# Seven pairs of eleven by seven products, weight sums on GpSimd, and a first block two rows of k at a time

## Chip, cores and metric

The kernel runs on one core of one Trainium2 chip. The metric is the time of one execution on the device, in microseconds (us), as the median of three runs; less is better.

The engines are named as the profile names them: PE is TensorE (matrix products), DVE is VectorE, ACT is ScalarE, POOL is GpSimd, SP only issues transfers.

## What is computed

A decoder trunk of two layers. Each layer does a half-step SwiGLU network, a mixer (a gated recurrence beside a spatial gating branch), and another half-step SwiGLU network, each followed by a layer norm. The change is about the first half of the four SwiGLU networks, `silu(x @ a) * (x @ b)`:

```python
D_MODEL, SEQ, DEPTH, D_FF = 1024, 512, 2, 2816
def swiglu(x, w13, w2):
    a, b = jnp.split(x @ w13, 2, axis=-1)
    return (jax.nn.silu(a) * b) @ w2
for l in range(DEPTH):
    x = layer_norm(ALPHA * x + 0.5 * swiglu(x, ffn1_w13[l], ffn1_w2[l]), ln_g[l, 0], ln_b[l, 0])
    m = mixer(x, w_in[l], ...)
    x = layer_norm(ALPHA * x + m, ln_g[l, 1], ln_b[l, 1])
    x = layer_norm(ALPHA * x + 0.5 * swiglu(x, ffn2_w13[l], ffn2_w2[l]), ln_g[l, 2], ln_b[l, 2])
```

## The kernel before

**Precision.** Every factor of a product is split into a high part (ACT copies it into a rounded type, L119) and a low part (DVE subtracts, L122). A product is then three matmuls: high by high, high by low, low by high.

**A network's first half.** The 2816 columns are 22 blocks of 128, each with a weight column `a` and one `b`. Blocks k and k+11 form pair k, so there are eleven pairs. A pair is done in one of two ways. *Plain* (`plain`, L147 and L593 to L594): two blocks, each with 24 matmuls for `a` and 24 for `b`, 512 columns wide. *By seven* (`seven_pair`, `product`, L548): the block matrix product of a pair in quarters, seven products in the place of eight, each of 24 matmuls with 256 moving columns. The seven products need sums of the weight quarters and sums of the x quarters. The x sums are made once for each network (`x_sums`, L471 to L490); the weight sums once for each pair.

**The order in a network.** Pairs 8, 9 and 10 (`front`) go plain, six blocks. Then pairs 0 to 5 (`by_seven`, `S_PAIRS = 6`) go by seven. Then pairs 6 and 7 (`behind`) go plain, four blocks. Then `Seven.run` makes the second half, also by seven products, from activation sums (`activation_sums`, L330 to L335: on DVE four subtractions of 256 columns and low parts of 256 and 512 columns) and from sums of the second weights.

**Weights of a pair by seven.** `weights_of_pair` loads two tiles `ra` (each a quarter of `a` beside a quarter of `b`), and `rc` and `rd`. On DVE it makes two sums `t13` (L521, 1024 columns), two of 512 columns into `t2` (L522) and one into `rc` (L526, 1024 columns). All seven factors of a pair are split before its first product stands. Seven evictions of PSUM banks A, B, C and E on DVE (L559 to L572) and three on ACT (L557, L565, L571) put the products together.

**Sums of the second weights.** `weight_sums` makes those of three pairs on DVE, in `front`. For the other eight, `sums_in_dram` (L288) has POOL's DMA queue copy and then add, DRAM to DRAM: four groups of two pairs, six steps a group, two transfers a step. Each step waits until the one before has landed. In the program the steps stand 6 us of counted PE time apart (`SUM_GAP`, counted by `flow.tick`).

**What sets the order.** A scheduler orders each engine's queue by the program's order and by when it believes operands are ready; `keep_in_program_order` pins an instruction to its place. Each queue is served strictly in order: an instruction that waits holds back all behind it on its engine.

**The start.** `first_block` (L1018 to L1043) loads quarters of the first weights and of x in turn, runs six matmuls on zeros while it waits (L1011), and then goes over k, for each k three matmuls for `a` and three for `b` (L1041).

Of the kernel before, what the change touches and what calls it, by code (L numbers as in the profile page):

```python
# [28 lines left out]
F32 = mybir.dt.float32  # L29
# [6 lines left out]
P = 128  # L36
D = 1024
T = 512
# [45 lines left out]
def trunk(ctx: ExitStack, tc, x_in, xt_in, w13, w2, w_in, w_br, w_out, ln_g, ln_b, lb_in, hgn, sgg, sgb, sgws,  # L84
# [33 lines left out]
    def split(hi, lo, src, pinned=False):  # L118
        act = S.activation(hi, src, AF.Copy)  # L119
        if pinned:  # L120
            tc.keep_in_program_order(act)
        V.tensor_tensor(lo, src, hi.bitcast(F32), op=ALU.subtract)  # L122
# [139 lines left out]
    class Seven:  # L262
# [51 lines left out]
        def activation_sums(self, k):  # L314

            r = self.r[k]
            x = wk.tile([P, 2, 256], F32, tag="sa", name="s12", bufs=NSA)
            if k >= self.KEPT:
                hi, lo = (quads(f"t{c}{k}", F32R) for c in "hl")
                parts = hi[:, 0], lo[:, 0], hi[:, 1:3], lo[:, 1:3]  # L320
            elif self.last is None:
                hi, lo = (quads(f"t{c}{k}", F32R) for c in "hl")
                self.last = hi, lo
                parts = hi[:, 0], lo[:, 0], hi[:, 1:3], lo[:, 1:3]
            else:
# [4 lines left out]
            V.tensor_tensor(x[:, 0], r[:, 2], r[:, 3], op=ALU.subtract)  # L330
            V.tensor_tensor(x[:, 1], r[:, 0], x[:, 0], op=ALU.subtract)
            split(parts[0], parts[1], r[:, 0])
            V.tensor_tensor(r[:, 2], r[:, 0], r[:, 2], op=ALU.subtract)
            V.tensor_tensor(r[:, 0], r[:, 1], x[:, 1], op=ALU.subtract)
# [155 lines left out]
    def raw_cd(w13_of, k, early=False):  # L490

        if early:
            rc, rd = slot(f"rc{k}"), slot(f"rd{k}")
        else:
            rc, rd = (wk.tile([P, 2, 512], F32, tag="rs", name=f"r{c}{k}", bufs=2) for c in "cd")
        for z, j in enumerate((k, k + NH2)):
            nc.sync.dma_start(rd[:, z], w13_of(NF + j)[:, H[0]])
            nc.sync.dma_start(rc[:, z], w13_of(j)[:, H[1]])
        return rc, rd

    def weights_of_pair(w13_of, k, rcd=None):

        js = (k, k + NH2)
        ra = [wk.tile([P, 2, 512], F32, tag="raw", name=f"r_p{j}", bufs=NRAW) for j in js]
        rc, rd = rcd or raw_cd(w13_of, k)
        t13 = [slot(f"t13{j}") for j in js]
        t2 = slot(f"t2{k}")
        for z, j in enumerate(js):
            wa, wb = w13_of(j), w13_of(NF + j)
            nc.sync.dma_start(ra[z][:, 0], wa[:, H[0]])  # L510
            nc.sync.dma_start(ra[z][:, 1], wb[:, H[1]])

        def parts(raw, name, early=False):
            hi, lo = ((slot(f"{v}_{name}", F32R) if early else
                       wk.tile([P, 2, 512], F32R, tag="w", name=f"{v}_{name}", bufs=NW)) for v in "hl")
            split(hi, lo, raw, early)
            return [(hi[:, z], lo[:, z]) for z in range(2)]

        p = [parts(ra[z], f"p{j}") for z, j in enumerate(js)]
        for z in range(2):  # L520
            V.tensor_tensor(t13[z], ra[z], rd[:, z:z + 1].broadcast_to([P, 2, 512]), op=ALU.add)  # L521
            V.tensor_tensor(t2[:, z], ra[z][:, 0], t13[z][:, 1], op=ALU.add)  # L522
        w2 = parts(t2, f"t2{k}")
        wt = [parts(t13[z], f"t{j}") for z, j in enumerate(js)]
        w21 = parts(rc, f"c{k}", True)
        V.tensor_tensor(rc, rc, t2, op=ALU.add)  # L526
        w4 = parts(rc, f"d{k}", True)
        return p, wt, w2, w21, w4

    def seven_pair(seven, s, k, w):  # L530

        p, wt, w2, w21, w4 = w
# [7 lines left out]
        def product(ps, units, c, first=True):  # L540
            for z in range(2):
                hi, lo = units[z]
# [9 lines left out]
        A, B, C, E = (bank(f"f{c}{k}") for c in "ABCE")  # L552
        r = seven.room(k).rearrange("p q t -> p (q t)")
        lower, upper = r[:, 0:512], r[:, 512:1024]
        b0, b1 = (wk.tile([P, T], F32, tag="sa", name=f"b{c}", bufs=NSA) for c in "01")
        product(A, [p[0][0], p[1][0]], "A11")
        S.activation(upper, A, AF.Copy)  # L557
        product(B, w2, "s2")
        V.tensor_tensor(upper, upper, B, op=ALU.subtract)  # L559
        product(C, [wt[0][0], wt[1][0]], "s1")  # L560
        V.tensor_tensor(b1, C, upper, op=ALU.subtract)
        product(E, [wt[0][1], wt[1][1]], "s3")
        V.tensor_tensor(b1, b1, E, op=ALU.subtract)
        product(A, w21, "A12", False)
        S.activation(lower, A, AF.Silu)  # L565
        product(C, [p[0][1], p[1][1]], "s4", False)
        V.tensor_tensor(b0, C, upper, op=ALU.subtract)
        V.tensor_tensor(lower, lower, b0, op=ALU.mult)
        product(E, w4, "A22", False)
        V.tensor_tensor(upper, E, upper, op=ALU.add)  # L570
        S.activation(upper, upper, AF.Silu)  # L571
        V.tensor_tensor(upper, upper, b1, op=ALU.mult)  # L572

    S_PAIRS = 6

    def ffn(l, i, last=False, first_of_all=False):
# [49 lines left out]
        for z, j in enumerate(js[2:]):  # L626
            args = blocks(j)
            if z == 3:
                w = weights_of_pair(w13_of, by_seven[0], rcd)
# [3 lines left out]
            if z == 1:  # L633
                rcd = raw_cd(w13_of, by_seven[0], True)
# [5 lines left out]
        for k in by_seven:  # L640
            seven_pair(seven, s, k, w if k == by_seven[0] else weights_of_pair(w13_of, k))
        due = [front[2:] + by_seven[:2], by_seven[2:5], by_seven[5:] + behind[:1], behind[1:]]
# [361 lines left out]
    def first_block(wa, wb):  # L1004
# [5 lines left out]
        for _ in range(6):  # L1010
            PE.matmul(idle[:, 0:P], zero[:, 0:P], zero[:, 0:P], start=True, stop=True)  # L1011
# [14 lines left out]
        feature(0, 0)  # L1026
        weight(1, 0)
        feature(0, 1)
# [8 lines left out]
        for k in range(KT):  # L1037
            mh, ml = from_x(k)
            for v in range(2):
                for i, (a, m) in enumerate(((w[v][0], mh), (w[v][0], ml), (w[v][1], mh))):  # L1040
                    PE.matmul(ps[v], a[:, k * P:(k + 1) * P], m, start=(k == 0 and i == 0),  # L1041
                              stop=(k == KT - 1 and i == 2))
            flow.tick(6 * MM)  # L1043
# [107 lines left out]
```

## Time and profile before

| | us |
|---|---|
| median of three runs | 2077.43 (2075.61 to 2080.03) |
| the profiled execution | 2075.15 |
| its span, first to last instruction | 2073.4 |
| DVE busy | 1465.6 (71%) |
| ACT busy | 871.3 (42%) |
| POOL busy | 284.7 (14%) |

The span's share is that of busy time; an engine can be busy and still not be what the end waits for. The pairs by seven of the first network lie between 75.0 and 195.9 us of the span, those of the others between 764.2 and 885.1, 1104.1 and 1225.0, and 1794.0 and 1914.9: four times 120.9 us. A row of the profile reads: line, engine, operation, output and inputs with their shapes, count, busy time and mean duration, idle time ahead of it and what ended that. In a list in order of time the first number is the start and the second the duration, both in us.

### The profile page before, as it was taken

Reading aid. Unit: us, or ns where it says so; the run is one execution under the profiler, and the core shown is the slowest. Engines: PE = TensorE matmul, PEld = TensorE weight load, DVE = VectorE, ACT = ScalarE, POOL = GpSimd, SP = SyncE. Lnnn points to the kernel's source line nnn. Section 1 sums busy time; section 2 is a strip of 40 time slices with the busy share of each in tenths; the row PEclk is TensorE's granted clock in tenths of the full one; section 3 lists DMA queues with packets and bytes.
Section 4 is the critical chain, followed back from the end, with each engine's and each line's share of the span. In section 5 each row is a group of like instructions: output and inputs, shape, how many; then the busy total and the mean of one; then the engine's idle time right before and its main releaser. Section 6 shows DMA issues by size and latency. Waiting matters only on the chain.

```text
span 2073.4 us, 30387 instructions
## 1 busy us (share of the span) xinstructions
PE 2058.6 (99%) x11764; PEld 1814.0 (87%) x11764; DVE 1465.6 (71%) x2285; ACT 871.3 (42%) x1219; POOL 284.7 (14%) x424
## 2 busy tenths in 40 slices
PE   9999999999999999999999999999999999999998
PEld 7999888888888989988899998888888888899886
DVE  7986878943535788777778878779444357987776
ACT  4443555234322434446534445542343224444453
POOL 1222002001000222210112220020010002122001
PEclk9999999999999999999999999999999999999999
DMA  8788677122243578867768886861222436788674
GB/s 300 226 236 205 194 267 250 42 82 82 82 156 98 205 222 218 210 172 275 238 219 244 219 216 194 275 209 52 82 90 84 143 97 237 218 217 218 178 264 141
DMA packets 142849, 381.27 MB, mean 184 GB/s; under 512 B 16624, under 2 KB 16880, under 8 KB 142704
## 3 DMA queue, kind: packets, MB, share of 16 engines
q1 hardware_dynamic: 100368, 258.13, 37.3%
q0 software_dynamic: 42336, 121.20, 22.7%
q8 instruction: 92, 1.51, 0.3%
q14 instruction: 53, 0.43, 0.1%
HBM read 344.66 MB, written 101.71 MB: 215 GB/s over the span
## 4 chain that ended last, share of the span: by engine, by line
PE 96%; DMA 2%; DVE 1%; ACT 1%; issue 0%; POOL 0%; SPq 0%; POOLq 0%; DVEq 0%; ACTq 0%
PE pa L147 9%; PE pb L147 9%; PE z L147 8%; PE fC L548 7%; PE fE L548 7%; PE fA L548 7%; PE pA L363 6%; PE pC L363 6%; PE y L229 4%; PE y L147 4%; PE fB L548 3%; PE pB L363 3%; PE pE L363 3%; PE pF L363 3%; PE q L147 2%; PE f L147 2%
## 5 line engine op out<-in xcount | busy, mean ns | idle before, releaser
L122 DVE TENSOR_TENSOR l_b<-r_b,h_b 128x1024 fp32r<-128x1024 f32 (+1 forms) x85 | 102.5, 1210 | 54.3 <-ACT h_b L119 53.8
L288 POOL DMA_DIRECT2D t<-in_w_dram x128 | 106.5, 885 | 215.5 <-DMA t<-in_w_dram 102.7
L147 PE MATMUL pa<-xh,l_a 128*128 128x512 f32 (+1 forms) x360 | 130.0, 361 | 1.0 <-DVE l_a L122 1.0
L147 PE MATMUL pa<-xl,h_a 128*128 128x512 f32 (+1 forms) x360 | 130.4, 362 | 0.5 <-DVE xl L122 0.5
L147 PE MATMUL pb<-xh,h_b 128*128 128x512 f32 (+1 forms) x360 | 130.3, 362 | 0.0
L147 PE MATMUL pa<-xh,h_a 128*128 128x512 f32 (+1 forms) x360 | 130.3, 362 | 0.0
L147 PE MATMUL pb<-xh,l_b 128*128 128x512 f32 (+1 forms) x360 | 129.9, 361 | 0.0
L147 PE MATMUL pb<-xl,h_b 128*128 128x512 f32 (+1 forms) x360 | 129.8, 361 | 0.0
L119 ACT ACTIVATE h_b<-r_b 128x1024 fp32r<-128x1024 f32 (+1 forms) x85 | 89.0, 1047 | 91.4 <-PE pa L147 34.1
L122 DVE TENSOR_TENSOR l_t<-t,h_t 128x1024 fp32r<-128x1024 f32 x72 | 87.3, 1222 | 42.1 <-ACT h_t L119 42.1
L119 ACT ACTIVATE h_t<-t 128x1024 fp32r<-128x1024 f32 x72 | 75.4, 1058 | 67.5 <-DVE t L522 49.1
L147 PE MATMUL z<-xh,h_z 128*128 128x512 f32 x256 | 102.6, 401 | 0.0
L147 PE MATMUL z<-xh,l_z 128*128 128x512 f32 x256 | 99.8, 390 | 0.0
L147 PE MATMUL z<-xl,h_z 128*128 128x512 f32 x256 | 99.8, 390 | 0.0
L122 DVE TENSOR_TENSOR l_z<-r_z,h_z 128x1024 fp32r<-128x1024 f32 x32 | 39.2, 1225 | 72.5 <-ACT h_z L119 72.4
L119 ACT ACTIVATE h_p<-r_p 128x1024 fp32r<-128x1024 f32 x48 | 50.4, 1058 | 69.5 <-PE fE L548 48.9
L147 PEld LDWEIGHTS pa<-xh,l_a 128*128 128x128 f32 x360 | 67.8, 188 | 11.7 <-DVE l_a L122 1.4
L147 PEld LDWEIGHTS pa<-xl,h_a 128*128 128x128 f32 x360 | 67.9, 189 | 11.4 <-DVE xl L122 1.2
L229 PE MATMUL y<-h_wo,yt 128*128 128x512 f32 x256 | 77.3, 392 | 0.0
L147 PEld LDWEIGHTS pa<-xh,h_a 128*128 128x128 f32 x360 | 67.9, 189 | 10.5 <-ACT xh L119 0.3
L147 PEld LDWEIGHTS pb<-xh,l_b 128*128 128x128 f32 x360 | 67.9, 189 | 10.4
L147 PEld LDWEIGHTS pb<-xl,h_b 128*128 128x128 f32 x360 | 67.9, 189 | 10.3
(363 smaller groups left out, 6704.2 us busy)
## 6 DMA issues: line engine op xcount, KB each, us to landing
t<-in_w_dram POOLq DMA_DIRECT2D x64, 512.0 KB, 9.1
r_p<-in_w_dram SPq DMA_DIRECT2D x96, 256.0 KB, 7.6
r_c<-in_w_dram SPq DMA_DIRECT2D x44, 512.0 KB, 5.8
r_d<-t SPq DMA_DIRECT2D x88, 256.0 KB, 4.2
r_a<-in_w_dram SPq DMA_DIRECT2D x39, 512.0 KB, 5.3
r_b<-in_w_dram SPq DMA_DIRECT2D x39, 512.0 KB, 5.5
t<-t POOLq DMA_DIRECT2D x76, 256.0 KB, 4.0
t<-in_w_dram POOLq DMA_DIRECT2D x64, 256.0 KB, 5.6
```

Of the source, the lines that this page charges most:

```text
L119: act = S.activation(hi, src, AF.Copy)
L122: V.tensor_tensor(lo, src, hi.bitcast(F32), op=ALU.subtract)
L147: PE.matmul(ps[:, n0:n0 + n], a[:, cs], m[:, n0:n0 + n], start=(i == 0), stop=(i == 3 * nk - 1))
L229: PE.matmul(ys[t][q], a[:, ts], m[:, q * 512:(q + 1) * 512], start=(k == 0 and i == 0), stop=(k == nk - 1 and i == 2))
L288: tc.keep_in_program_order(nc.gpsimd.dma_start(*of(k), **kw))
L363: PE.matmul(ps[tt], a[:, ts], m, start=(start and k == 0 and z == 0), stop=(stop and k == NH2 - 1 and z == 2), skip_group_check=not start)
L548: PE.matmul(ps[:, half[z]], a[:, ms], v, start=start, stop=(m == 3 and i == 2), skip_group_check=not (first and z == 0))
```

## The change

1. `S_PAIRS` is 7: pairs 0 to 6 go by seven, and only pair 7 plain behind them (two blocks in the place of four).
2. The weights of a pair come as quarters a, b, c, d (`PairWeights`), for both blocks of the pair at once. Four sums of 1024 columns give all that the products need: t = a + b, then b = d + b, then a = a + b, then c = a + c. They run on POOL (`sum`), in the same queue as the transfers of `sums_in_dram`. `weights_of_pair`'s five sums on DVE go.
3. The pairs run as one stream of steps (`seven_pairs`), a step being one product in the order of `ORDER`. At step n stand the evictions of product n-1, the split of the factor for product n+3 (`AHEAD`), and the loads and sums of the next pair at fixed steps. Evictions, splits and sums are pinned to that order. The eviction of the second product (C) moves from DVE to ACT, as a copy.
4. Of the activation sums, three (`due`: those of pair 10, pair 0 and pair 1) move into the stream, in its pairs 0, 2 and 3. The other six stay behind it.
5. In the first block twelve matmuls on zeros stand in the place of six, the second quarter of x is loaded ahead of the first of `b`, and the matmuls go over k two at a time: six for `a`, then six for `b`.

```diff
-    def split(hi, lo, src, pinned=False):
-        act = S.activation(hi, src, AF.Copy)
-        if pinned:
-            tc.keep_in_program_order(act)
-        V.tensor_tensor(lo, src, hi.bitcast(F32), op=ALU.subtract)
+    def pin(ins):
+        if pinned[0]:
+            tc.keep_in_program_order(ins)
+    def split(hi, lo, src):
+        pin(S.activation(hi, src, AF.Copy))
+        pin(V.tensor_tensor(lo, src, hi.bitcast(F32), op=ALU.subtract))
...
+    ORDER = (("A", "A11", "a"), ("C", "s1", "t"), ("A", "A12", "c"), ("E", "s3", "b"), ("B", "s2", "a"),
+             ("C", "s4", "d"), ("E", "A22", "c"))
+    AHEAD = 3
+    class PairWeights:
+        def load(self, to, col, row):
+            for z, j in enumerate((self.k, self.k + NH2)):
+                nc.sync.dma_start(to[:, z], self.w13_of(col + j)[:, H[row]])
+        def split(self):
+            src = ORDER[len(self.parts)][2]
+            hi, lo = (wk.tile([P, 2, 512], F32R, tag="w", name=f"{v}_p{src}_{self.k}", bufs=NW) for v in "hl")
+            split(hi, lo, getattr(self, src))
+            self.parts.append((hi, lo))
+        def sum(self, to, u, v):
+            to, u, v = (getattr(self, n) for n in (to, u, v))
+            pin(G.tensor_tensor(to, u, v, op=ALU.add))
...
+        def evictions(k, m):
+            if m == 0:
+                pin(S.activation(upper, b["A"], AF.Copy))
+            elif m == 2:
+                pin(S.activation(lower, b["A"], AF.Silu))
+            elif m == 1:
+                b["b1"] = wk.tile([P, T], F32, tag="sa", name="b1", bufs=NSA)
+                pin(S.activation(b["b1"], b["C"], AF.Copy))
+            elif m == 3:
+                pin(V.tensor_tensor(b["b1"], b["b1"], b["E"], op=ALU.subtract))
+            elif m == 4:
+                pin(V.tensor_tensor(upper, upper, b["B"], op=ALU.subtract))
+                pin(V.tensor_tensor(b["b1"], b["b1"], upper, op=ALU.subtract))
+            elif m == 5:
+                b0 = wk.tile([P, T], F32, tag="sa", name="b0", bufs=NSA)
+                pin(V.tensor_tensor(b0, b["C"], upper, op=ALU.subtract))
+                pin(V.tensor_tensor(lower, lower, b0, op=ALU.mult))
+            elif m == 6:
+                pin(V.tensor_tensor(upper, b["E"], upper, op=ALU.add))
+                pin(S.activation(upper, upper, AF.Silu))
+                yield
+                pin(V.tensor_tensor(upper, upper, b["b1"], op=ALU.mult))
...
+            if m == 0:
+                banks[k] = {c: bank(f"f{c}{k}") for c in "ABCE"}
+                pws[k].sum("c", "a", "c")
+            if m == 2:
+                for v in due.get(k, ()):
+                    seven.activation_sums(v)
+            if m == 0 and nk is not None:
+                pws[nk] = weights_of(nk)
+                pws[nk].load_d()
+            elif m == 1 and nk is not None:
+                pws[nk].load_c()
+            elif m == 2 and nk is not None:
+                pws[nk].sum("t", "a", "b")
+            elif m == 3 and nk is not None:
+                pws[nk].sum("b", "d", "b")
+            c, mov, _ = ORDER[m]
+            if m == 5 and nk is not None:
+                pws[nk].sum("a", "a", "b")
+            product(banks[k][c], pws[k].parts[m], mov, c == "B" or m in (0, 1, 3))
...
-    S_PAIRS = 6
+    S_PAIRS = 7
...
-        due = [front[2:] + by_seven[:2], by_seven[2:5], by_seven[5:] + behind[:1], behind[1:]]
+        seven_pairs(seven, s, by_seven, weights_of, pw, {0: [front[2]], 2: by_seven[0:1], 3: by_seven[1:2]})
+        due = [by_seven[2:5], by_seven[5:] + behind]
...
-        for _ in range(6):
+        for _ in range(12):
             PE.matmul(idle[:, 0:P], zero[:, 0:P], zero[:, 0:P], start=True, stop=True)
...
         feature(0, 0)
+        feature(0, 1)
         weight(1, 0)
-        feature(0, 1)
...
-        for k in range(KT):
+        for k, v in ((k + z, v) for k in range(0, KT, 2) for v in range(2) for z in range(2)):
```

How the change moves instructions is seen in two queues. First POOL, in the third group of the transfers that make the sums of the second weights in DRAM (t_82 and t_83 are the first sums of two pairs, t_89 and t_90 the second sums, t_99 and t_100 the third). Before, nothing stands between them:

```order
L288 DMA t_82<-in_w_dram 256x512
L288 DMA t_83<-in_w_dram 256x512
L288 DMA t_82<-in_w_dram 256x1x512
L288 DMA t_83<-in_w_dram 256x1x512
L288 DMA t_89<-t_82 128x512
L288 DMA t_90<-t_83 128x512
L288 DMA t_89<-in_w_dram 128x512
L288 DMA t_90<-in_w_dram 128x512
```

With the change the sums of the weight quarters of two pairs stand between them (ra, rb, rc, rd are the quarters, rt is t):

```order
L293 DMA t_82<-in_w_dram 256x512
L293 DMA t_83<-in_w_dram 256x512
L534 TENSOR_TENSOR ra_1451<-ra_1451,rb_1452 128x1024
L293 DMA t_82<-in_w_dram 256x1x512
L293 DMA t_83<-in_w_dram 256x1x512
L534 TENSOR_TENSOR rc_630<-ra_1451,rc_630 128x1024
L293 DMA t_89<-t_82 128x512
L293 DMA t_90<-t_83 128x512
L534 TENSOR_TENSOR rt<-ra_1698,rb_1699 128x1024
L534 TENSOR_TENSOR rb_1699<-rd_1704,rb_1699 128x1024
L293 DMA t_89<-in_w_dram 128x512
L293 DMA t_90<-in_w_dram 128x512
```

A sum that the products wait for now stands behind transfers that themselves wait for the landing of the transfers ahead of them.

Second DVE, in the middle of the stream. Before, sums of weights (L521, L522, L526) stand between the low parts (L122) and the evictions (L567 to L572):

```order
L521 TENSOR_TENSOR t_1163<-r_p_1155,rd_1157 128x1024
L563 TENSOR_TENSOR b_969<-b_969,fE_966 128x512
L122 TENSOR_TENSOR l_p_1174<-r_p_1155,h_p_1173 128x1024
L522 TENSOR_TENSOR t_1164<-r_p_1155,t_1163 128x512
L122 TENSOR_TENSOR l_t_1182<-t_1164,h_t_1181 128x1024
L122 TENSOR_TENSOR l_t_1186<-t_1162,h_t_1185 128x1024
L567 TENSOR_TENSOR b_968<-fC_965,r_967 128x512
L122 TENSOR_TENSOR l_t_1190<-t_1163,h_t_1189 128x1024
L568 TENSOR_TENSOR r_967<-r_967,b_968 128x512
L570 TENSOR_TENSOR r_967<-fE_966,r_967 128x512
```

With the change one low part follows each step's evictions, and in the third pair (number 2) the activation sums of pair 0 (L335 to L339, r_753 is its room) stand between two of them:

```order
L583 TENSOR_TENSOR r_1003<-fE_968,r_1003 128x512
L127 TENSOR_TENSOR l_pb_1196<-rb_971,h_pb_1195 128x1024
L586 TENSOR_TENSOR r_1003<-r_1003,b_1037 128x512
L127 TENSOR_TENSOR l_pa_1243<-ra_970,h_pa_1242 128x1024
L127 TENSOR_TENSOR l_pd_1275<-rd_976,h_pd_1274 128x1024
L335 TENSOR_TENSOR s_1278<-r_753 128x256
L336 TENSOR_TENSOR s_1278<-r_753,s_1278 128x256
L127 TENSOR_TENSOR tl_1280<-r_753,th_1279 128x256
L338 TENSOR_TENSOR r_753<-r_753 128x256
L339 TENSOR_TENSOR r_753<-r_753,s_1278 128x256
L127 TENSOR_TENSOR tl_1280<-s_1278,th_1279 128x512
L127 TENSOR_TENSOR l_pc_1316<-rc_630,h_pc_1315 128x1024
```

The sums of weights are gone from this queue, and three times in a network an activation sum has come into it.

More of the change, by code (lines that the diff above doesn't have):

```diff
@@ L561, in seven_pair @@
[L561 to L571, printed above, removed]
@@ new lines, in ahead @@
+        def ahead(n):
+            if n < last:
+                k, m = at(n)
+                pws[k].split()
+        for n in range(last):
+            k, m = at(n)
+            nk = k + 1 if n + 7 < last else None
+            ev = evictions(*at(n - 1)) if n else iter(())
+            for _ in ev:
+                ahead(n + AHEAD)
+                break
+            else:
+                ahead(n + AHEAD)
+            for _ in ev:
+                pass
+            if m == 0:
[17 more added lines that the diff above has]
+            product(banks[k][c], pws[k].parts[m], mov, c == "B" or m in (0, 1, 3))
@@ L576, in ffn @@
+        for _ in evictions(*at(last - 1)):
+            pass
+    S_PAIRS = 7
     def ffn(l, i, last=False, first_of_all=False):
@@ L628, in ffn @@
             if z == 3:
-                w = weights_of_pair(w13_of, by_seven[0], rcd)
+                t = slot("rt")
+                cs = [slot(f"rc{v}") for v in range(2)]
+                weights_of = lambda k: PairWeights(w13_of, k, t, cs[k % 2])
+                pinned[0] = True
+                pw = weights_of(by_seven[0])
+                pw.load_c()
+                pw.load_d()
+                pw.sum("t", "a", "b")
+                pw.split()
+                pw.sum("b", "d", "b")
+                pw.split()
+                pw.sum("a", "a", "b")
+                pw.split()
+                pinned[0] = False
             plain(j, args)
```

94 lines of the change are left out of this document (34 added, 60 removed).

## The prediction

> **What bounds the kernel now.** First the page's busy times and granted clock, then who made PE wait, then the chain of work that ended last.
>
> ```profile
> PE 2058.6 (99%) x11764; PEld 1814.0 (87%) x11764; DVE 1465.6 (71%) x2285; ACT 871.3 (42%) x1219; POOL 284.7 (14%) x424
> PEclk9999999999999999999999999999999999999999
> ```
>
> ```profile
> PE pa L1041 <- ACT xh L119: 1.4, 1, 1.4
> PE idle L1011 <- DVE zero L1008: 1.1, 1, 1.1
> PE pa L147 <- DVE l_a L122: 1.0, 1, 1.0
> PE pb L1041 <- ACT h_b L119: 0.7, 1, 0.7
> PE pa L147 <- DVE xl L122: 0.5, 1, 0.5
> ```
>
> A busy PE need not be PE at its peak, but here the second view says the same: in 2073.4 us PE waits 4.7 us (total, times, longest), nearly all of it at the start, at full clock. So the time is the sum of the matmuls, and two things alone can change it: fewer matmuls, or waits that do not exist now. The chain gives the price of a product by seven and of half a plain block:
>
> ```profile
> 74.95 2.87 PE fA L548 x24
> 77.82 2.88 PE fB L548 x24
> 80.70 2.88 PE fC L548 x24
> ...
> 195.90 5.47 PE pa L147 x24
> 201.37 5.44 PE pb L147 x24
> ```
>
> Start to start, 24 matmuls of 256 columns take 2.88 us and 24 of 512 columns 5.44 us. Busy times of the stages (PE, PEld, DVE, ACT, POOL, then clock, DMA share, GB/s) show who stands near the limit beside PE:
>
> ```profile
> 75.00:195.90 120.90, 120.90 (x1009) 120.90 (x1008) 99.60 (x111) 53.73 (x60) 27.20 (x38) 1.00 0.85 215
> 195.90:239.50 43.60, 43.60 (x194) 36.07 (x193) 30.41 (x62) 17.28 (x30) 6.02 (x9) 1.00 0.61 176
> 239.50:340.00 100.50, 100.50 (x452) 83.07 (x451) 80.54 (x107) 58.09 (x76) 10.85 (x17) 1.00 0.80 269
> ```
>
> In the six pairs by seven (first row) PE never rests, DVE is at 99.6 of 120.9 us and the DMA engines at 0.85.
>
> **The matmuls.** A plain pair is 4 x 5.44 = 21.76 us, a pair by seven 7 x 2.88 = 20.16 us. One pair in each of four networks changes: 4 x 1.60 = 6.4 us less on PE. From the profiled execution: 2075.15 - 6.4 = 2068.75 us. The median lies 2077.43 - 2075.15 = 2.28 us above it, so 2071.0 us if nothing new waits. Every other part is asked only whether it makes PE wait.
>
> **DVE and ACT in the stream.** The groups of the first network's six pairs:
>
> ```profile
> L122 DVE TENSOR_TENSOR l_t<-t,h_t 128x1024 fp32r<-128x1024 f32 x16 | 19.5, 1223 | 9.2 <-ACT h_t L119 9.2
> L521 DVE TENSOR_TENSOR t<-r_p,rd 128x1024 f32<-128x1024 f32 x10 | 12.2, 1219 | 0.0
> L522 DVE TENSOR_TENSOR t<-r_p,t 128x512 f32<-128x512 f32 x10 | 6.8, 683 | 0.0
> L568 DVE TENSOR_TENSOR r<-r,b 128x512 f32<-128x512 f32 x6 | 4.1, 686 | 0.0
> L119 ACT ACTIVATE h_t<-t 128x1024 fp32r<-128x1024 f32 x15 | 15.8, 1058 | 14.2 <-DVE t L522 10.8 <-PE fC L548 3.2
> L557 ACT ACTIVATE r<-fA 128x512 f32<-128x512 f32 x6 | 3.5, 580 | 0.0
> ```
>
> DVE before, a pair: seven low parts 8.5, three sums of 1024 columns (L526's counted at L521's duration) 3.7, two of 512 1.4, seven evictions 4.8; 18.4 of 20.16 us. The five sums go: 13.3 us. ACT has seven high parts (7.4) and, with the new copy, four evictions (2.4): 9.8 us. An activation sum brings DVE five operations of 256 columns and one of 512:
>
> ```profile
> L330 DVE TENSOR_TENSOR s<-r x44: 417/421/427, 32.0 to 1959.4; 128x256 f32<-128x256 f32 x44
> L122 DVE TENSOR_TENSOR tm<-s,tm x16: 683/686/691, 213.3 to 1962.0; 128x512 fp32r<-128x512 f32 x16
> ```
>
> 5 x 0.42 + 0.69 = 2.8 us, and 16.1 us in the pairs that hold one: room. What waits now: an eviction waits for its product at the head of its queue, and behind it stands the split for the product three steps on. That split has 3 x 2.88 = 8.64 us, needs 1.06 + 1.22 = 2.3, and so the pinned order hides, at a cost of nothing on PE. If a split came later than those 6.3 us of cover, PE would wait for the rest, four times over.
>
> Behind the stream six activation sums (16.8) and two blocks (each 2 x 1.22 + 0.69, together 6.3) make 23.1 us of DVE in 21.8 us, where now 43.6 us hold nine and four. Some 1 to 6 us, with the next weights' splits, spill into the second half, whose DVE has 20 us free in 100.5 (third row above); its first weights stand ahead of the sums in the queue. I take nothing; the bound is 0 to 6 us a network.
>
> **The sums on POOL.** No row shows POOL adding 1024 columns. The nearest is a fill, on the same engine and in the same type:
>
> ```profile
> L744 POOL MEMSET sc<- 128x512 f32 x8 | 4.1, 538 | 29.3 <-PE q L147 17.4 <-PE f L147 12.0
> L288 POOL DMA_DIRECT2D t<-in_w_dram x128 | 106.5, 885 | 215.5 <-DMA t<-in_w_dram 102.7 <-DMA t<-t 91.1 <-issue 21.1
> L288 POOL DMA_DIRECT2D t<-t x64 | 35.2, 550 | 223.2 <-DMA t<-in_w_dram 217.6 <-issue 5.6
> ```
>
> One stream of 1024 columns is 1.08 us there; a sum has three (two in, one out), so 1.1 to 3.2 us. I take two, 2.15 us, since the fill is the nearest row and an addition has at least its output's stream and one more. Four sums are 8.6 us a pair; the transfers' issues are (106.5 + 35.2) / 192 = 0.74 us each, and 6.6 of them fall in 20.16 us (a step of two each 6.12 us): 4.9. POOL is busy 13.5 of 20.16 us. Loads come earlier than they are used, since two pairs' quarters fit, and their bytes for a pair are the same. Taken: nothing on PE. By the Trainium skill (GPSIMD Engine Reference, section 3.1) an addition of 2048 float32 elements was measured at 4497 ns, an estimate of 2.25 us for 1024; POOL would then be busy 13.9 us, and the sum would not change.
>
> **The first block.** PE begins it at 5.44 and ends at 19.08 us, 13.6 us for 48 matmuls that take 10.9 at 5.44/24 each, so at most 2.7 us can go. Six more matmuls on zeros can cost 1.5 us (six take 2.93 us, from 4.00 they would end at 6.93 instead of 5.44). Neither reaches the end:
>
> ```profile
> 1.07 2.93 PE L1011 MATMUL idle<-zero 128*128 128x128 f32 x12 [1.07 <-DVE zero L1008]
> 5.44 0.79 PE L1041 MATMUL pa<-xh,h_a 128*128 128x512 f32 x1 [1.44 <-ACT xh L119]
> ...
> 18.85 0.39 PE L1041 MATMUL pb<-xh,l_b 128*128 128x512 f32 x1
> ```
>
> ```profile
> 2.10 4.93 DMA xt<-in_xt_dram
> ...
> 14.62 6.56 DMA r_a<-in_w_dram
> ...
> 43.57 4.54 DVE xr L471 x4
> ...
> 62.95 1.23 DVE l_a L122
> ...
> 64.22 5.29 PE pa L147 x22
> ```
>
> At 64.22 PE waits 1.0 us for a low part at the end of a chain of loads and then a full DVE; no PE stands in that chain before 64. An earlier PE waits longer there. Taken: 0; bounds -2.7 and +0.5 us.
>
> **Rival 1: the sums wait behind transfers.** POOL serves in order, and the transfers wait for each other's landing (first of the network's first step, and second of the third group's third step):
>
> ```profile
> 63.53 1.15 POOL L288 DMA_DIRECT2D t<-in_w_dram  x2
> ...
> 160.63 0.55 POOL L288 DMA_DIRECT2D t<-t  x1 [1.97 <-DMA t<-in_w_dram]
> ```
>
> From the first step's second issue (64.1) that is 96.5 us. Now the first step starts 11 us before the stream; with the change it stands behind a sum that waits for a split at the stream's beginning, so some 2 us into it. The third group's third step then ends 98.5 us into the stream, and pair 5's first sum, which the program has at step 30 (86.4 us), comes 12.1 us late. It can: its product is six steps on (17.28), less 2.15, 1.06 and 1.22 leaves 12.85 us. The cover is 0.7 us. Landings 1 to 2 us slower make PE wait that long in each network; 1.5 us gives 2071 + 6 = 2077 us. For: POOL waits in half of that stage already. Against: other sums have 3 to 7 us of cover.
>
> **Rival 2, slower: POOL and DVE shut each other out.** POOL's small operation, with DVE idle (DVE's last ended at 504.44) and beside a DVE operation with both inputs in SBUF:
>
> ```profile
> 503.75 0.69 DVE L878 TENSOR_REDUCE ms<-o 128x4 f32<-128x512 f32 x1 [2.36 <-ACT o L876]
> 504.53 0.19 POOL L173 TENSOR_SCALAR rs<-ms 128x4 f32<-128x4 f32 x1 [40.43 <-DVE ms L878]
> ...
> 509.66 1.22 DVE L122 TENSOR_TENSOR l_z<-r_z,h_z 128x1024 fp32r<-128x1024 f32 x1
> 509.81 1.12 POOL L173 TENSOR_SCALAR vr<-vq 128x1 f32<-128x1 f32 x1 [0.85 <-ACT sq L945]
> ```
>
> 0.19 us becomes 1.12 and ends 0.05 us behind DVE's: POOL waited for DVE. If DVE waits for POOL's sums in the same way, low parts (8.5), three evictions without PSUM (2.1) and four sums (8.6) share 20.16 us: 19.2 fits, but with an activation sum it is 22.0, 1.84 too many. Three such pairs in four networks: 22 us, 2093 us. Bounds: 0, if the splits' cover takes it, and, if all of DVE waits, 13.3 + 8.6 - 20.16 = 1.75 a pair, 20.6 a network with the activation sums, 83 us. It decides from sums of (20.16 - 13.4)/4 = 1.7 us in those pairs, 2.4 in the others. Against: POOL hardly reads SBUF now, so no row shows DVE waiting. The Trainium skill (SBUF — State Buffer, Who interferes with whom) states the whole: a VectorE instruction with two SBUF inputs and a GpSimd instruction that reads SBUF exclude each other, whichever starts first; the trace agrees in one direction, and no run here shows the other. By its 2.25 us it would be 2071 + 27 = 2098 us.
>
> **Rival 3:** the first block does more than I say, if the chain to 64 moves with PE: 2071 - 1.5 = 2069.5 us.
>
> **How the numbers follow.** Forecast 2071.0 us, chance 0.48; its own range, with the runs' spread of about 2 us, is 2069 to 2073.2. Rival 1, 0.22; rival 2, 0.25, since half of it is seen in the trace but its excess is small enough for the cover to take; rival 3, 0.05. A measurement of this kernel tells about 0.2% from no change: 2073.3 to 2081.6 is the same. Faster: forecast and rival 3, 0.53. Same: rival 1, 0.22. Slower: rival 2, 0.25. The range goes from 2069 to 2094, which leaves out the heavier half of rival 2 and little below.
>
> **What would show it.** Right: four stages by seven of 7 x 20.16 = 141.1 us, no PE wait on a split, low parts on DVE still at 1.22 us. Rival 1: POOL's sums idle behind a landing, then ACT's high part waits for POOL and PE for that. Rival 2: DVE's operations longer than 1.22 and 0.69 us and PE waiting on DVE low parts after pairs 0, 2 and 3. Rival 3: no wait near 64 us, and the stream begins before 74.95. The forecast is wrong if PE waits over 2.2 us in all four networks together, or if the second half opens with a wait.

## The result and the profile after

| | before | after |
|---|---|---|
| median of five runs, us | 2077.43 | 2138.63 (2136.03 to 2143.62) |
| ratio, 95% interval | | 1.0294 [1.0277, 1.0312] |
| profiled span, us | 2073.4 | 2137.8 |

The change costs 61 us. The forecast was 2071.0 us and the range ended at 2094. The page of the changed kernel (busy time, share of the span, instructions) and the list of who made PE wait (total, times, longest, us):

```profile
PE 2069.9 (97%) x12064; PEld 1831.4 (86%) x12064; DVE 1570.1 (73%) x2197; ACT 889.3 (42%) x1263; POOL 572.6 (27%) x536
```

```profile
PE fA L554 <- ACT r L567: 28.9, 17, 3.8
PE fB L554 <- DVE l_pa L127: 12.3, 8, 1.9
PE fE L554 <- ACT h_pt L126: 8.3, 5, 1.9
PE pa L152 <- DVE l_a L127: 3.0, 1, 3.0
```

PE, which waited 4.7 us in all, now waits over 52 us in these rows alone, and nearly all of it inside the streams of products. DVE, which lost five sums a pair, is busy 104 us longer. The four streams (their windows: PE, PEld, DVE, ACT, POOL busy, then clock, DMA share, GB/s):

```profile
77.50:234.00 156.50, 144.66 (x1177) 142.99 (x1176) 138.94 (x117) 65.10 (x82) 97.32 (x72) 0.99 0.79 198
783.50:939.50 156.00, 143.35 (x1178) 141.59 (x1177) 138.74 (x117) 65.09 (x82) 97.36 (x72) 1.00 0.78 198
1138.10:1297.20 159.10, 146.15 (x1178) 144.54 (x1177) 140.75 (x117) 65.09 (x82) 97.28 (x72) 0.98 0.77 195
1844.50:2001.10 156.60, 143.70 (x1177) 141.66 (x1176) 139.43 (x117) 65.10 (x82) 97.32 (x73) 1.00 0.77 199
```

Seven pairs at 20.16 us are 141.1 us; here they take 156 to 159. Together that is 63.7 us more than four times 141.0. The first stream also begins 2.7 us later than before (its first matmul at 77.48 against 74.79), some 4.4 us are lost outside the streams, and 6.4 us are saved: 63.7 + 2.7 + 4.4 - 6.4 = 64.4 us, the difference of the spans. Of the 63.7 us some 50 are in the rows of waits above. The rest shows as PE's busy time, which in the four windows is 13.5 us above four times 141.1; a part of that is a lower clock (0.99 and 0.98 in two of the windows).

One stretch of the first stream shows how the loss looks (start, duration, engine, line, operation):

```profile
122.35 3.47 DVE L581 TENSOR_TENSOR r<-r,b 128x512 f32<-128x512 f32 x1
122.59 2.68 POOL L534 TENSOR_TENSOR ra<-ra,rb 128x1024 f32<-128x1024 f32 x1
...
125.75 1.21 DVE L127 TENSOR_TENSOR l_pc<-rc,h_pc 128x1024 fp32r<-128x1024 f32 x1
126.89 0.68 DVE L583 TENSOR_TENSOR r<-fE,r 128x512 f32<-128x512 f32 x1
...
127.59 0.63 ACT L584 ACTIVATE r<-r 128x512 f32<-128x512 f32 x1 [8.88 <-DVE r L583]
128.13 1.04 ACT L126 ACTIVATE h_pb<-rb 128x1024 fp32r<-128x1024 f32 x1
129.08 0.58 ACT L567 ACTIVATE r<-fA 128x512 f32<-128x512 f32 x1
```

The eviction L581, 0.69 us by itself, takes 3.47 us and ends 0.55 us behind POOL's sum. DVE's next evictions come late for it, ACT waits 8.88 us at the head of its queue for one of them, and the eviction of bank A (L567) stands behind that. PE needs this bank read out before it adds the pair's third product to it. This is the row PE fA <- ACT r of the list above. Not all of the 8.88 us is loss: with the sums on DVE (below) ACT's wait at this place is 6.1 us in the mean (42.4 us in seven).

### The profile page after: what moved, and what is told of

It is laid out like the page before. It is cut to its first block, busy times and chain, and to the rows that moved or that the text cites. A ratio compares the mean times of both kernels' runs of the same rounds, so it can differ in the third digit from the quotient of the medians.

```text
span 2137.8 us, 31318 instructions
## 1 busy us (share of the span) xinstructions
PE 2069.9 (97%) x12064; PEld 1831.4 (86%) x12064; DVE 1570.1 (73%) x2197; ACT 889.3 (42%) x1263; POOL 572.6 (27%) x536
## 5 line engine op out<-in xcount | busy, mean ns | idle before, releaser
L127 DVE TENSOR_TENSOR l_pa<-ra,h_pa 128x1024 fp32r<-128x1024 f32 x56 | 108.1, 1930 | 3.0 <-ACT h_pa L126 3.0
L152 PE MATMUL pb<-xh,h_b 128*128 128x512 f32 (+1 forms) x296 | 105.4, 356 | 0.0
L152 PE MATMUL pb<-xh,l_b 128*128 128x512 f32 (+1 forms) x296 | 105.0, 355 | 0.0
L152 PE MATMUL pb<-xl,h_b 128*128 128x512 f32 (+1 forms) x296 | 104.9, 355 | 0.0
L127 DVE TENSOR_TENSOR l_pc<-rc,h_pc 128x1024 fp32r<-128x1024 f32 x56 | 83.8, 1496 | 24.4 <-ACT h_pc L126 24.4
L554 PE MATMUL fA<-xh,h_pc 128*128 128x256 f32 x224 | 67.5, 301 | 28.9 <-ACT r L567 28.9
L534 POOL TENSOR_TENSOR rb<-rd,rb 128x1024 f32<-128x1024 f32 x28 | 83.9, 2995 | 8.9 <-DMA rd<-in_w_dram 7.6
L534 POOL TENSOR_TENSOR ra<-ra,rb 128x1024 f32<-128x1024 f32 x28 | 70.8, 2527 | 38.2 <-DVE l_pa L127 37.8
L534 POOL TENSOR_TENSOR rt<-ra,rb 128x1024 f32<-128x1024 f32 x28 | 80.8, 2884 | 0.3
L127 DVE TENSOR_TENSOR l_pb<-rb,h_pb 128x1024 fp32r<-128x1024 f32 x28 | 51.8, 1850 | 39.5 <-ACT h_pb L126 39.5
```

The lines of the kernel that those rows point to most:

```text
L127: pin(V.tensor_tensor(lo, src, hi.bitcast(F32), op=ALU.subtract))
L152: PE.matmul(ps[:, n0:n0 + n], a[:, cs], m[:, n0:n0 + n], start=(i == 0), stop=(i == 3 * nk - 1))
L534: pin(G.tensor_tensor(to, u, v, op=ALU.add))
L554: PE.matmul(ps[:, half[z]], a[:, ms], v, start=start, stop=(m == 3 and i == 2), skip_group_check=not (first and z == 0))
```

## Experiments

Four theories stood at the start. **L**: a sum on POOL and a DVE operation with two inputs in SBUF shut each other out, both ways (rival 2 of the prediction); below this is called the lock. **T**: the sums come late because they stand behind waiting transfers on POOL (rival 1). **A**: the activation sums overload DVE in the stream. **O**: the pinned order itself makes queues wait. "Stream" below is the time from a stream's first product to the end of its last, lowest to highest of the four networks.

### Sums on DVE

```diff
-            pin(G.tensor_tensor(to, u, v, op=ALU.add))
+            pin(V.tensor_tensor(to, u, v, op=ALU.add))
```

> The changed kernel with the four weight sums of a pair on VectorE in the place of GpSimd; order, loads and transfers as they are. Theory L (lock: a sum on GpSimd and a DVE operation with both inputs in SBUF shut each other out, in both directions): DVE then holds 13.3 + 4 x 1.22 = 18.2 us of a pair's 20.16, 21.0 in the three pairs with an activation sum, 135.9 us of the 141.1 us of a stream; the streams fall from 156 to 159 us to 141 to 145, the time to 2070 to 2090 us. Theory T (the sums come late because they stand behind waiting transfers on GpSimd): the same fall, so this run does not part L from T. Theory A (the activation sums in the stream are too much for DVE even without a lock): DVE has more to do than before, no fall, 2135 to 2160 us. Theory O (the pinned order makes an eviction wait at the head of a queue): no fall, 2130 us or more.

Measured: 2074.15 us, ratio to the kernel before 0.9976 [0.9964, 0.9987]; streams 141.1 to 141.2 us. This edit alone gives back 64 us. A and O fall as causes by themselves: the order and the activation sums are the same, and DVE has more to do. L and T stand.

### No transfers on POOL

```diff
-  copies = (lambda k: (self.t13[k], w[k][:, 0:3:2]), lambda k: (t2[k], self.t13[k][:, 1]),
-            lambda k: (self.t4[k], t2[k]))
+  copies = (lambda k: (self.t13[k], w[k][:, 0:3:2]), lambda k: (t2[k], w[k][:, 0]),
+            lambda k: (self.t4[k], w[k][:, 3]))
...
-  tc.keep_in_program_order(nc.gpsimd.dma_start(*of(k), **kw))
+  if of is copy:
+      tc.keep_in_program_order(nc.sync.dma_start(*of(k)))
```

> The changed kernel with no transfer for the sums of the second weights on GpSimd's queue: the copies of each group go from SyncE, straight from the weights, and the additions are left out, so these sums are not computed; the weight sums stay on GpSimd. Theory L: the streams stay at 150 to 159 us, the time at 2115 to 2139 us. Theory T: the sums come on time, streams of 141 to 143 us, time 2070 to 2080 us. Theories A and O: no change, 2130 to 2140 us.

Measured: 2114.36 us; streams 151.1 to 151.5. Without the transfers that make the second weights' sums 10 us a stream stay lost: T alone isn't enough. (Two stores of pair 10's activation sum stay on POOL's queue in this run; they matter below.) The 24 us that came back say that it has a part.

### Fills in the place of the sums

```diff
-            pin(G.tensor_tensor(to, u, v, op=ALU.add))
+            for _ in range(2):
+                pin(G.memset(to, 0.0))
```

> The changed kernel with each weight sum on GpSimd replaced by two fills of the same 1024 columns with zero (2 x 1.08 us = 2.15 us beside 2.4 us of a sum, with no input from SBUF), so the weight sums are not computed. GpSimd's queue and its transfers stay. Theory L (an instruction that reads SBUF is needed on GpSimd for the lock): DVE's low parts are 1.22 us again beside the fills, streams 141 to 144 us, time 2070 to 2085 us. Theory T: the fills still stand behind the transfers, streams 150 us or more, 2110 to 2139 us. Theory A: no change, 2130 to 2140 us. If a fill locks as a sum does: 2115 to 2139 us, and DVE's operations stretched beside the fills.

Measured: 2099.35 us; streams 146.3 to 151.2. The groups between 770 and 900 us, in the second network's stream (busy us, mean ns of one | idle before):

```profile
L127 DVE TENSOR_TENSOR l_pc<-rc,h_pc 128x1024 fp32r<-128x1024 f32 x13 | 15.9, 1222 | 12.6 <-ACT h_pc L126 12.6
L535 POOL MEMSET ra<- 128x1024 f32 x12 | 12.8, 1065 | 0.3
```

DVE's low parts are back at 1.22 us: fills don't hold DVE. Yet 5 to 10 us a stream are lost. Who made PE wait in this run:

```profile
PE fA L555 <- ACT r L568: 11.7, 7, 2.3
PE fC L555 <- ACT h_pt L126: 4.7, 3, 2.5
PE fC L555 <- DVE l_pt L127: 3.0, 5, 0.8
```

By their times the waits lie in two pairs of a stream only, pair 2 and pair 5. All three waits for h_pt, the high part of t, are in pair 5.

So the expectation of neither theory was met whole: both causes are real, and each was thought to be all.

### All activation sums behind the stream

```diff
-        seven_pairs(seven, s, by_seven, weights_of, pw, {0: [front[2]], 2: by_seven[0:1], 3: by_seven[1:2]})
+        seven_pairs(seven, s, by_seven, weights_of, pw, {})
...
-        due = [by_seven[2:5], by_seven[5:] + behind]
+        due = [front[2:] + by_seven[:4], by_seven[4:] + behind]
```

> The changed kernel with all nine activation sums behind the stream, none in it; the weight sums stay on GpSimd. Theory L: DVE's two-input operations and the sums need 7 x 1.22 + 3 x 0.69 + 4 x 2.4 = 20.2 us of a pair's 20.16 without any activation sum, so part of the loss stays: streams of 143 to 152 us, time 2085 to 2120 us, with up to 8 us a network of it given back behind the stream. Theory A: streams of 141 us, time 2071 to 2085 us. Theory T: streams of 150 us or more, 2120 to 2139 us.

Measured: 2125.52 us; streams 149.3 to 151.7. The activation sums are no more the whole cause than the transfers.

### Fills, and no transfers

The edits of the second and third run in one.

> Both changes of the two runs before in one: each weight sum replaced by two fills, and no transfer for the second weights' sums on GpSimd's queue, so neither the weight sums nor those of the second weights are computed. If the lock (10 us a stream without transfers) and the queue behind the transfers (7 us a stream without the lock) are all there is: every stream 141.1 to 141.3 us, no PE wait in them, the time 2066 to 2076 us. If the pinned order or the activation sums cost anything by themselves: streams of 143 us or more, and PE waiting on ACT or DVE in them.

Measured: 2075.21 us; streams 140.9 to 141.0. Nothing is left inside the stream with both causes gone, so neither the pinned order nor the activation sums cost there by themselves. Nor does a store that makes POOL wait. Pair 10's is still in the stream, and POOL stands almost 12 us before it, with the fills behind:

```profile
90.11 0.54 POOL L347 DMA_DIRECT2D th<-th  x1 [11.81 <-ACT th L126]
```

What this time has above 2071 us lies outside the streams. In the profiled execution (2079.24 us; the eight lie between 2071.24 and 2079.69) the first stream begins at 79.60 us in the place of 74.79, from the new start (below), and some 5 us are lost between the first stream and the second.

### Sums on DVE, and the first block as before

> The changed kernel with the weight sums on DVE and with the first block as it was before (six matmuls on zeros, loads and matmuls in the old order). If the new first block costs time (it leaves the low part that PE needs near 64 us where it was or later, PE waits 2.0 us for it in the place of 1.0, and the clock is halved for 3.4 us behind that wait): 1 to 4 us below the run with the sums on DVE, 2070 to 2073 us. If the new first block gains: 1 to 3 us above it, 2075 to 2078 us. If it does neither: 2074 us.

Measured: 2070.78 us (2068.34 to 2073.55), ratio 0.9968 [0.9956, 0.9981]; streams 141.1 to 141.2. The first row is the first stream's window, the second a DVE group of low parts in the second network's stream:

```profile
74.90:216.10 141.20, 141.20 (x1176) 141.03 (x1175) 125.09 (x142) 68.37 (x85) 32.69 (x44) 1.00 0.83 214
```

```profile
L127 DVE TENSOR_TENSOR l_pa<-ra,h_pa 128x1024 fp32r<-128x1024 f32 x13 | 15.8, 1218 | 0.0
```

This version is 0.3% below the kernel before, and the interval excludes no difference. Its median is 3.4 us below that of the run that differs from it only in the first block, but the two were measured on different chips. Against the kernel before beside each they are 7.1 and 4.5 us lower, and the intervals overlap.

### The new first block alone

> The kernel before with the new first block alone. If it costs time: 1 to 4 us above the kernel before, with a PE wait of 2 us or more near 64 us and half the clock behind it. If it gains: up to 2.7 us below. If it does neither, within 1 us.

Measured: 2082.87 us, ratio 1.0024 [1.0014, 1.0034], 5 us above the kernel before. The wait, and the windows behind it (in them the last three numbers are clock, DMA share, GB/s):

```profile
PE pa L147 <- DVE l_a L122: 4.3, 1, 4.3
```

```profile
64.00:66.00 2.00, 0.00 (x0) 0.00 (x0) 2.00 (x4) 2.00 (x3) 1.80 (x5) 0.72 0.81 309
66.00:68.00 2.00, 1.97 (x5) 1.59 (x6) 2.00 (x3) 0.13 (x1) 0.47 (x1) 0.50 1.07 290
68.00:70.00 2.00, 2.00 (x6) 1.55 (x5) 2.00 (x3) 0.00 (x0) 0.00 (x0) 0.50 0.87 301
70.00:72.00 2.00, 2.00 (x7) 1.55 (x6) 1.97 (x3) 0.00 (x0) 0.00 (x0) 0.58 0.92 259
```

PE waits 4.3 us in the place of 1.0, and then runs at half clock for nearly 7 us, which costs another 3.4 us. The low part itself is late, by a change of order on DVE. Before, and with the new block:

```profile
25.90 0.69 DVE L311 TENSOR_TENSOR ra_w<-ra_w 128x512 f32<-128x512 f32 x1
...
26.65 0.69 DVE L311 TENSOR_TENSOR rb_w<-rb_w,ra_w 128x512 f32<-128x512 f32 x1
27.26 1.22 DVE L122 TENSOR_TENSOR l_a<-r_a,h_a 128x1024 fp32r<-128x1024 f32 x1
```

```profile
25.97 0.68 DVE L311 TENSOR_TENSOR ra_w<-ra_w 128x512 f32<-128x512 f32 x1
26.57 1.22 DVE L122 TENSOR_TENSOR l_a<-r_a,h_a 128x1024 fp32r<-128x1024 f32 x1
27.71 0.68 DVE L311 TENSOR_TENSOR rb_w<-rb_w,ra_w 128x512 f32<-128x512 f32 x1
```

The sum of rb_w is 1.06 us later, for a low part went ahead of it. Its store and the next load into that buffer follow it, and DVE waits for this load at 41.62 us (39.82 before). From there DVE is full until the low part at 64. The first block itself does end earlier, at 17.7 us against 19.2, so that PE has the longer to wait. In all the first stream begins 4.4 us later (79.23 against 74.79).

### Seven pairs, and nothing else

```diff
-    S_PAIRS = 6
+    S_PAIRS = 7
...
-        due = [front[2:] + by_seven[:2], by_seven[2:5], by_seven[5:] + behind[:1], behind[1:]]
+        due = [front[2:] + by_seven[:4], by_seven[4:] + behind]
```

> The kernel before with seven pairs by seven and nothing else of the change; the nine activation sums are divided over the two plain blocks that are left behind the pairs, five and four. From 28 matmul groups by 2.88 us in the place of 16 by 5.44: 4 x 1.6 = 6.4 us less on PE, 2072 us if nothing waits. Behind the pairs DVE then has nine activation sums (25.2 us) and two blocks (6.3 us) in 21.8 us: if the second half waits for what is late, up to 6 us a network, 2072 to 2096 us. If the stream's order (steps, split three ahead) is needed to hold seven pairs, PE waits inside the pairs too, more than 141.3 us for seven of them.

Measured: 2082.97 us, ratio 1.0023 [1.0014, 1.0033]. Seven pairs take 140.9 to 141.0 us in the old code too. The loss is behind them, where nine activation sums have two blocks: the second half (pB, pE, pA) now waits for their parts, 8.4 us in these rows:

```profile
PE pB L363 <- ACT h_t L119: 5.4, 4, 1.6
PE pE L363 <- DVE l_d L122: 1.6, 3, 1.1
PE pB L363 <- DVE l_t L122: 1.4, 4, 0.3
```

So the stream isn't needed to hold the products, but room for activation sums inside it is: the run with the sums on DVE and the old start, which has three of them there, has no such row.

### Three fills in the place of a sum, and no transfers

> Three fills of 1024 columns (3.2 us) in the place of each weight sum, longer than the 2.4 us of a sum, and no transfer for the second weights' sums on GpSimd; neither kind of sum is computed. If the loss without transfers (streams of 151 us with the sums on GpSimd) came from sums that take too long there: streams of 145 us or more. If it came from the lock with DVE: streams of 141.0 to 141.5 us, DVE's low parts at 1.22 us beside the fills.

Measured: 2074.85 us; streams 140.9 to 141.0, with DVE as short as ever:

```profile
L127 DVE TENSOR_TENSOR l_pa<-ra,h_pa 128x1024 fp32r<-128x1024 f32 x13 | 15.9, 1222 | 4.3 <-ACT h_pa L126 4.3
```

Its fills and, of the changed kernel, a sum on POOL (shortest, median, longest of one in ns):

```profile
L536 POOL MEMSET ra<- x84: 946/954/959, 71.1 to 1912.8; 128x1024 f32 x84
```

```profile
L534 POOL TENSOR_TENSOR ra<-ra,rb x28: 2397/2402/2999, 73.0 to 1976.6; 128x1024 f32<-128x1024 f32 x28
```

Three fills hold POOL for 2.9 us (3 x 0.95), longer than a sum of 2.40, and cost nothing. It isn't the sums' length on POOL that costs.

### Sums on POOL, without transfers and without activation sums

> The weight sums on GpSimd with neither the transfers (the second weights' sums are not computed) nor an activation sum in the stream (all nine behind it). If only the operations that lock are shared time (7 x 1.22 + 3 x 0.69 + 4 x 2.4 = 20.2 us of a pair's 20.16): streams of 141 to 143 us. If operations of DVE that need no lock queue behind one that waits for it, so that nearly all of DVE's 13.3 us adds to the sums' 9.6 us (22.9 us a pair): streams of 147 to 160 us. If the loss without transfers was the activation sums' alone: 141.1 us.

Measured: 2085.14 us; streams 140.9 to 141.0. (What the time has above 2075 us is mostly lost in the second half, as in the run with seven pairs alone.) The lock is there all the same, in both directions:

```profile
102.89 1.23 DVE L127 TENSOR_TENSOR l_pb<-rb,h_pb 128x1024 fp32r<-128x1024 f32 x1 [1.65 <-ACT h_pb L126]
102.94 3.44 POOL L535 TENSOR_TENSOR rt<-ra,rb 128x1024 f32<-128x1024 f32 x1
...
104.03 2.90 DVE L587 TENSOR_TENSOR r<-r,b 128x512 f32<-128x512 f32 x1
```

The sum starts beside a low part and takes 3.44 us, 1.0 more than its 2.4: it waits until DVE is through at 104.12. Then DVE's next operation, 0.69 us by itself, takes 2.90 and ends at 106.93, 0.55 behind the sum's end. The Trainium skill (SBUF — State Buffer, section Who interferes with whom) says that whichever of the two is first shuts out the other, and that a GpSimd instruction that only writes doesn't: the sums here and the fills above agree with both. PE waits for none of it. The locked work, 20.2 us by the sum of its parts, is about what a pair takes on PE (20.16); the 0.05 us that are over can hide in the covers.

### Fills and transfers, activation sums behind

> Two fills in the place of each weight sum (which is not computed), the transfers on GpSimd's queue as in the change, but all nine activation sums behind the stream. The parts of pair 10's sums are stored from GpSimd's queue, and in the stream that store waited 7 to 10 us for the high part, with the fills behind it. If the 7 us a stream that the queue costs come from this store, which starts the chain of transfers late: streams of 141 to 143 us. If they come from the landings that the chain of transfers waits for all along: streams of 146 us or more.

Measured: 2087.10 us (again with the second half waiting); streams 140.9 to 141.0. With fills in the place of the sums, the queue behind the transfers costs nothing in the stream when no activation sum stands in it.

### Fills and transfers, only pair 10's activation sum behind

```diff
-        seven_pairs(seven, s, by_seven, weights_of, pw, {0: [front[2]], 2: by_seven[0:1], 3: by_seven[1:2]})
+        seven_pairs(seven, s, by_seven, weights_of, pw, {2: by_seven[0:1], 3: by_seven[1:2]})
...
-        due = [by_seven[2:5], by_seven[5:] + behind]
+        due = [front[2:] + by_seven[2:5], by_seven[5:] + behind]
```

> Two fills in the place of each weight sum (not computed), the transfers on GpSimd's queue, the activation sums of pairs 0 and 1 in the stream as in the change, and only that of pair 10, whose parts GpSimd stores, behind it. If the store in the stream (it waits 9 to 10 us at the head of GpSimd's queue, and the fills and the chain of transfers stand behind it) is what the fills lose with the transfers (streams of 146 to 151 us): streams of 141.0 to 141.5 us. If it is DVE's time for activation sums in any pair: streams of 144 us or more.

Measured: 2072.81 us; streams 141.0 in all four. The activation sums of pairs 0 and 1 are in the stream here and cost nothing, so DVE's time for an activation sum doesn't explain the loss. What pair 10's has beside theirs is the store of its parts, here in the second network of the run with fills and everything else:

```profile
772.24 1.14 POOL L293 DMA_DIRECT2D t<-in_w_dram  x2
782.41 0.56 POOL L346 DMA_DIRECT2D th<-th  x1 [9.03 <-ACT th L126]
783.48 0.54 POOL L346 DMA_DIRECT2D tl<-tl  x1 [0.51 <-DVE tl L127]
784.01 1.98 POOL L535 MEMSET rt<- 128x1024 f32 x2
```

POOL stands 9 us before a store whose data come only in the middle of pair 0, and the next pair's sums and the chain of transfers start that much later. The chain's second step is issued at 785.94 us, 14.0 us into the stream; without the store it comes 4.1 us into it (774.00). The store costs only together with that chain: without the transfers POOL waited before it even longer (11.81 us, above), and no PE time was lost.

## Why the prediction was wrong

The runs side by side, by the four things that differ inside the stream:

| weight sums | transfers on POOL | activation sums in the stream | stream, us |
|---|---|---|---|
| sums on POOL | yes | yes | 155.8 to 158.9 |
| sums on POOL | yes | none | 149.3 to 151.7 |
| sums on POOL | no | yes | 151.1 to 151.5 |
| sums on POOL | no | none | 140.9 to 141.0 |
| fills on POOL | yes | yes | 146.3 to 151.2 |
| fills on POOL | yes | none, or not pair 10's | 140.9 to 141.0 |
| fills on POOL | no | yes | 140.9 to 141.0 |
| sums on DVE | yes | yes | 141.1 to 141.2 |

**The matmuls: right.** 6.4 us less was the whole gain to be had. With the sums on DVE and the old start it comes out: 2070.78 us against a forecast of 2071.0, and 7.1 us below the kernel before that was measured beside it. That agreement speaks for this term alone, since the forecast had the sums on POOL and the new start.

**DVE, ACT and the pinned order: right as long as nothing holds DVE.** The splits' cover of 6.3 us holds, even with DVE at 125 of 141.2 us. But it isn't the shortest cover, and the prediction named no other. The copy of bank A stands between a pair's first and third product, so it has one product less its own time: 2.88 - 0.58 = 2.3 us, by an estimate. What I let spill behind the stream costs little: with the sums on DVE and the new start, PE waits 1.9 us in all for parts of the second half.

**The sums on POOL, "taken: nothing on PE": this step failed.** It counted POOL's time and not what POOL's reading does to DVE, and put that into a rival. The rival had the mechanism and the pairs right and was priced too low, in two ways. A sum takes 2.40 us, not 2.15, so that a pair with an activation sum holds 13.4 + 9.6 = 23.0 us of locked work, 2.84 too many in the place of 1.84; three pairs in four networks make 34 us, and the runs without transfers lost 41. And it reckoned that the splits' cover of 6.3 us might take the excess. An excess of 2.84 us a pair is less than that, but more than bank A's 2.3. In the streams without transfers PE waits 1.6 us for this bank right behind each of the pairs 0, 2 and 3, and 0.8 us for a low part two products later. The low parts were the sign that the prediction gave; the larger wait is one that it did not have. Its own upper bound for this rival was 83 us, and the 61 us lie below that: the stated range left this half out.

**Rival 1: right in kind and in one of two places, wrong in size.** I priced it at pair 5 and 1.5 us a network. The fills show 7.3 us a network (29.4 us in four). In pair 5 it comes as forecast: the first sum (t) is late, ACT's high part (h_pt) waits for it and PE for that. Bank A's wait in pairs 2 and 5 comes on top. What I left out is a part of a moved step: the activation sum of pair 10 takes its two stores (L341 before, L346 now) into the stream, on POOL's queue, and they wait for their data ahead of the sums and of the chain of transfers.

**The rivals weren't alternatives.** I gave each its own time and chance, as if one of them would come. They spend the same slack: the sums' lock alone leaves none (20.2 of 20.16 us), and then either late sums or activation sums turn into waits. With no activation sum in the stream the lock alone and the transfers alone cost nothing there, and both together 8 to 11 us. How they lose these 8 to 11 us was not taken further apart. With the activation sums in the stream lock and transfers lost 63.7 us together, where the lock without transfers lost 41 and the queue without the lock 29.

**The first block, "taken: 0; bounds -2.7 and +0.5": wrong.** It costs 5.0 us alone. With the sums on DVE it costs 3.4 us by the medians, of which the profiled executions show 1.1 us at the start (the first stream begins at 75.95 against 74.90); where the rest comes from stays open. I had read that the end of PE's wait near 64 us hangs on loads and DVE, which holds, and took DVE's order there as given. The scheduler set it anew. And I had no price for a wait's aftermath, the halved clock.

## What to carry to other kernels

Before work is moved to GpSimd, add its time with SBUF inputs to DVE's time with two SBUF inputs, as if both were one engine, pair by pair and not as a mean over a stage. For a queue that serves in order, list all that the change puts on it, stores of moved steps included, and ask of each when its data are ready. Where several rivals eat the same slack, price them together.

## What the runs showed of the hardware

It was not POOL's work as such but its reading that held DVE: fills left it alone. And of DVE's operations only those with two inputs in SBUF were held. Two evictions of the same size in the first stream of the changed kernel, the second with one input in PSUM:

```profile
L577 DVE TENSOR_TENSOR b<-b,r 128x512 f32<-128x512 f32 x7 | 16.6, 2376 | 0.2
L583 DVE TENSOR_TENSOR r<-fE,r 128x512 f32<-128x512 f32 x6 | 4.1, 682 | 0.0
```

2.38 us in the mean against 0.68. Over the four streams the evictions with an input in PSUM (L574, L576, L580, L583; 28 of each) never took more than 0.69 us, and those with both inputs in SBUF (L577, L581, L586) up to 3.45, 3.55 and 3.64 us.

The clock was halved behind some PE waits, and stayed so for several us after the wait was over. With the new first block alone it was 0.50 behind a wait of 4.3 us (above); with the sums on DVE a wait of 2.0 us was enough:

```profile
PE pa L152 <- DVE l_a L127: 2.0, 1, 2.0
```

```profile
66.00:68.00 2.00, 2.00 (x6) 1.54 (x6) 1.75 (x2) 1.06 (x1) 0.00 (x0) 0.50 1.01 357
```

The length of one wait doesn't decide it. With fills and no transfers two waits near 715 us, 1.15 and 0.66 us long, had it halved behind them (0.74, 0.50 and 0.90 in the three windows from 716 to 722, 3.4 us at half clock):

```profile
715.45 0.38 PE L152 MATMUL pa<-xh,h_a 128*128 128x256 f32 x1 [1.15 <-ACT xh L126]
716.49 0.39 PE L152 MATMUL pa<-xl,h_a 128*128 128x256 f32 x1 [0.66 <-DVE xl L127]
```

```profile
718.00:720.00 2.00, 2.00 (x11) 2.00 (x11) 1.90 (x4) 0.49 (x1) 1.10 (x3) 0.50 0.68 249
```

In the second stream of the changed kernel a wait of 2.59 us left it full:

```profile
834.91 0.39 PE L554 MATMUL fA<-xh,h_pc 128*128 128x256 f32 x1 [2.59 <-ACT r L567]
```

```profile
836.00:838.00 2.00, 2.00 (x19) 2.00 (x18) 2.00 (x3) 1.54 (x3) 1.69 (x2) 1.00 0.78 58
```

Behind the wait of 1.0 us before the change it stayed full too, and so it did in the streams without transfers, whose longest wait is 1.6 us:

```profile
PE fA L555 <- ACT r L568: 18.8, 12, 1.6
```

```profile
778.80:930.00 151.20, 143.51 (x1177) 141.53 (x1176) 135.10 (x117) 65.32 (x82) 69.36 (x27) 1.00 0.47 156
```

The Trainium skill (TensorE: Matmul & The Clock Gate, Part 1) has the clock fall after an idle window of about 3.4 us; here 2.0 us did it. What decided between these waits the runs don't show.
